# Early inputs in another order, and GpSimd beside VectorE for some of the early splits

## The chip, the cores and the metric

The kernel runs on one core of one Trainium2 chip. The metric is device time in microseconds (us); a time stated for a kernel is the median of its runs. TensorE multiplies, ScalarE and VectorE do the elementwise work, GpSimd (POOL in the profile) does very little here, and SyncE (SP) issues most of the DMA transfers.

## The reference

One decoder layer for two request groups: 256 prompt tokens and 8 sequences of 4 sample tokens, 288 tokens in all, in float32, with a model width of 4096.

```python
mod = jax.nn.silu(c) @ w_ada + b_ada
shift, scale, gate = jnp.split(mod, 3, axis=-1)
h = x * (1 + scale[:, None]) + shift[:, None]
q, k, v, z_a, u, v_b, z_b, g_a, g_b = split_cols(h @ w_in)
# A = sliding-window attention with sinks * silu(z_a)
# B = u * (masked chunk mixing of LN(v_b) + b_s) * silu(z_b)
merged = jax.nn.sigmoid(g_a) * (attn @ w_pa) + jax.nn.sigmoid(g_b) * (out_b @ w_pb)
y = merged @ w_o
x = layer_norm(ALPHA * x + gate[:, None] * y, ln_g, ln_b)
```

c has 9 rows: one for the prompt, one for each sample sequence. Part of the output are also the new key, value and v_b rows.

## The kernel before, in words

Tokens lie along the free dimension (288 columns) and the model width along the partitions, in 32 tiles of 128. The weights are streamed: a `Unit` is one DMA of up to 128 x 2048 float32 values (1 MB) on SyncE's queue into one of five `raw` buffers (L174). For the products every weight is split into a high part and a low part: for each half of a unit, ScalarE casts raw into `wH` (L182) and VectorE subtracts it from raw to get `wL` (L183), both with three buffers of 128 x 1024. The activations are split in the same way, h into `hH` (L298) and `hL` (L299). `prod` then issues three matmuls for each block of 128 x 128: wH with hH (L194), wH with hL (L195), wL with hH (L196).

The conditioning product silu(c) @ w_ada needs no split: `ada_units` multiplies the raw weights with `cT`, the transposed c, padded to 32 columns for each tile (L234). It is worked off in nine chunks of the model width, `CHUNKS` = 1, 2, 2, 2, 1, 4, 4, 8, 8 tiles. When the last conditioning unit of a chunk is done, `ada_fin` copies the result out of PSUM (`adae`, L250), transposes it on TensorE with the identity `ident` (`adaT`, L257), adds the bias `bada` (L280, L281), adds 1 to the scale (L287), modulates that chunk of x in place in the buffer `xs` (L292 for the prompt, L295 and L296 for the samples), makes hH and hL, and calls `load_x` for the next chunk of x (L270, ScalarE's queue), into the same place.

56 column tiles of w_in are worked on early ("early units", `ea` in the profile), while the conditioning still runs: as soon as a chunk of h is there, `early_units` multiplies it with the 56 column tiles and adds the PSUM result onto accumulators in SBUF (`accA`, `accB`, `xs`, `Q`). For chunk 0 the results are copied, by VectorE (L342) and ScalarE (L340) in turn; for later chunks VectorE adds (L344). PSUM holds three such results (`ps_acc`, three buffers). A unit of a chunk of n tiles holds 16 / n column tiles, so a result is complete after 3n matmuls.

The order of units is written out by `first_order`: the four conditioning units of chunk 0, two early units of chunk 0, three conditioning units of chunk 1, and so on, with two early units of the previous chunk kept for the time in which the next chunk's modulation is under way. `run` starts each unit (its DMA and its splits) two units ahead of the one whose matmuls are being issued. The framework under the kernel assigns the instructions to each engine's stream by this program order and its own estimate of when each can run, so the streams can differ from the text: matmuls of two units can stand mixed in TensorE's stream. Each engine then works its stream off in order.

After the early part come the remaining columns of w_in, attention and chunk mixing beside them, then the products with w_pa, w_pb and w_o, and the final layer normalisation, where GpSimd takes part (L869, L877).

The constants are loaded at the start on ScalarE's queue, each with its own DMA: cT, `ident`, `bada`, `lngb` (gain and bias of the last normalisation), then the first chunk of x.

Of the kernel before, what the change touches and what calls it, by code (L numbers as in the profile page):

```python
# [10 lines left out]
F32 = mybir.dt.float32  # L11
F32R = mybir.dt.float32r
AF = mybir.ActivationFunctionType
ALU = mybir.AluOpType
# [4 lines left out]
P = 128  # L19
# [91 lines left out]
def build(ctx, tc, nc, I, O):  # L111
# [17 lines left out]

    ident = const.tile([P, P], F32, name="ident")  # L130
    cT = const.tile([P, KT, 32], F32, name="cT")
    bada = const.tile([P, 96], F32, name="bada")
    lngb = const.tile([P, 2, KT], F32, name="lngb")
    gate = const.tile([P, KT, 9], F32, name="gate")
    epst = const.tile([P, 1], F32, name="epst")
    nc.scalar.dma_start(cT, I["cT"])
    nc.scalar.activation(cT, cT, AF.Silu)  # L137
    nc.scalar.dma_start(ident, I["ident"])
    nc.scalar.dma_start(bada, I["bada"])
    nc.scalar.dma_start(lngb, I["lngb"])  # L140
    nc.vector.memset(epst, EPS)

    hH = [slot(f"hH{i}", dt=F32R) for i in range(2)]
# [23 lines left out]
    class Unit:  # L167
        def __init__(self, src, body, split=True, blocks=16):
            self.src, self.body, self.split, self.blocks = src, body, split, blocks

        def start(self):
            raw = wp.tile([P, UNIT], F32, tag="raw", name="raw", bufs=RAW)
            w = self.blocks * P
            nc.sync.dma_start(raw[:, :w], self.src[:, :w])  # L174
            self.raw = raw
            self.H, self.L = [], []
            if self.split:
                for hf in range(w // 1024):
                    s = raw[:, hf * 1024:(hf + 1) * 1024]
                    h = wp.tile([P, 1024], F32R, tag="wH", name="wH", bufs=HB)  # L180
                    lo = wp.tile([P, 1024], F32R, tag="wL", name="wL", bufs=HB)
                    nc.scalar.copy(h, s)  # L182
                    nc.vector.tensor_sub(lo, s, h.bitcast(F32))  # L183
                    self.H.append(h)
                    self.L.append(lo)
# [12 lines left out]
    def run(items, ahead=2):  # L198
# [5 lines left out]
        for x in items:  # L204
            if not isinstance(x, Unit):
                x()
                continue
            while started < len(units) and started < k + 1 + ahead:
                units[started].start()
                started += 1  # L210
            x.body(x)
            k += 1
# [54 lines left out]

    def load_x(c):
        n, o = CHUNKS[c], OFFS[c]
        nc.scalar.dma_start(xs[:, 0, :n], I["xT"][:, o:o + n])  # L270

    def ada_fin(c):
        n, o = CHUNKS[c], OFFS[c]

        def modulate(blocks):
# [12 lines left out]
            for k in range(0, n, HSTEP):  # L288
                w = min(HSTEP, n - k)
                x = xs[:, 0, k:k + w]  # L290
                for i in range(w):
# [7 lines left out]
                nc.vector.tensor_sub(hL[a][:, b:b + w], x, hH[a][:, b:b + w].bitcast(F32))  # L299
            if c + 1 < len(CHUNKS):  # L300
                load_x(c + 1)
            h_done.add(c)
# [63 lines left out]
    def early_units(c):  # L366
# [17 lines left out]
        def unit(j):  # L384
            es = range(j * per, min(NE, (j + 1) * per))
            return Unit(I["we"][base + j], body_for(j, es), blocks=len(es) * n)
        return [unit(j) for j in range(count[c])]

# [501 lines left out]
    items = []  # L890
    load_x(0)

# [39 lines left out]
def layout(x_prompt, x_sample, cache_k, cache_v, c_prompt, c_sample, w_ada, b_ada, w_in, attn_sinks,  # L932
# [6 lines left out]
    c[0], c[1:9] = c_prompt[0], c_sample  # L939
    A["cT"] = f(c.reshape(32, KT, P).transpose(2, 1, 0))  # L940
    A["ident"] = np.eye(P, dtype=np.float32)
    A["bada"] = f(b_ada[0].reshape(96, P).T)
    A["gbrow"] = f(np.stack([ln_gain[0], ln_bias[0]]))
    A["lngb"] = f(np.stack([ln_gain[0], ln_bias[0]]).reshape(2, KT, P).transpose(2, 0, 1))

# [72 lines left out]
```

## Time and profile before

| | before |
|---|---|
| median of 3 runs | 3072.95 us (3072.71 to 3073.15) |
| profiled execution | 3071.9 us |
| its span | 3070.1 us |
| its mean granted TensorE clock | 0.994 |
| DMA over the span | 700.09 MB, 228 GB/s |
| VectorE busy | 1571.7 us (51%) |
| GpSimd busy | 15.4 us (1%) |

The span runs from the first to the last instruction that the profile shows. Shares are of the span. In the groups and the timeline each instruction has its engine, its line, what it writes and reads, and in brackets how long its engine stood idle before it and what ended that. A matmul counts as busy to its modelled end, so neighbours overlap: the distance of their starts is what one takes. Queue instructions (SPq, ACTq) only issue a DMA.

### The profile page before, as it was taken

The numbers are of one execution on the slowest core, as the hardware profiler recorded it, in microseconds if no ns is written. First come the engines' busy times: TensorE is split into PE (matmuls) and PEld (weight loads), VectorE is DVE, ScalarE is ACT, GpSimd is POOL, SyncE is SP. The second block draws the span as 40 slices with busy tenths as digits, with TensorE's granted clock in tenths as the row PEclk, the third lists the DMA queues.
The fourth block names the chain that finished last, engine by engine and source line by source line (L and its number), as shares of the span: only waits on it lengthen the run. The fifth ranks groups of instructions, "written<-read, shape, count | busy, mean of one in ns | idle before, by whom it ended". The sixth has DMA issues, their size and how long they took to land.

```text
span 3070.1 us, 53574 instructions
## 1 busy us (share of the span) xinstructions
PE 3030.2 (99%) x23168; PEld 2850.6 (93%) x23168; DVE 1571.7 (51%) x2262; ACT 1078.1 (35%) x1381; POOL 15.4 (1%) x14
## 2 busy tenths in 40 slices
PE   7999999999999999999999999999999999999998
PEld 6887888888999999999999999999999999999997
DVE  4777554444445545454444643444555555555555
ACT  3222223322333434343333333333444444433333
POOL 0000000000000000000000000000000000000001
PEclk9999999999999999999999999999999999999998
DMA  8888877877767565555555555666565555555552
GB/s 327 332 322 321 340 278 286 315 267 285 271 244 249 186 218 206 210 214 189 212 206 206 206 215 215 221 217 220 186 229 188 188 188 188 175 176 177 177 177 95
DMA packets 128673, 700.09 MB, mean 228 GB/s; under 512 B 14835, under 2 KB 44819, under 8 KB 49299
## 3 DMA queue, kind: packets, MB, share of 16 engines
q1 hardware_dynamic: 109584, 669.56, 60.0%
q10 hardware_dynamic: 18852, 27.10, 2.5%
q8 instruction: 182, 2.98, 0.4%
q14 instruction: 55, 0.44, 0.0%
HBM read 676.85 MB, written 19.46 MB: 227 GB/s over the span
## 4 chain that ended last, share of the span: by engine, by line
PE 95%; DVE 1%; DMA 1%; issue 0%; ACT 0%; DVEq 0%; ACTq 0%
PE in L194 13%; PE in L196 13%; PE in L195 13%; PE ea L194 8%; PE ea L195 7%; PE ea L196 7%; PE ada L234 5%; PE p L194 5%; PE y L194 5%; PE y L196 4%; PE p L196 4%; PE p L195 4%; PE y L195 4%; DVE wL L183 0%; PE pT L518 0%
## 5 line engine op out<-in xcount | busy, mean ns | idle before, releaser
L182 ACT CAST wH<-raw 128x1024 fp32r<-128x1024 f32 x848 | 884.6, 1048 | 1856.9 <-PE in L195 649.8
L183 DVE TENSOR_TENSOR wL<-raw,wH 128x1024 fp32r<-128x1024 f32 x848 | 1033.7, 1224 | 981.7 <-ACT wH L182 981.2
L194 PE MATMUL in<-hH,wH 128*128 128x288 f32 x2944 | 881.0, 299 | 0.0
L195 PE MATMUL in<-hL,wH 128*128 128x288 f32 x2944 | 869.7, 295 | 0.0
L196 PE MATMUL in<-hH,wL 128*128 128x288 f32 x2944 | 865.8, 294 | 0.0
L194 PEld LDWEIGHTS in<-hH,wH 128*128 128x128 f32 x2944 | 551.7, 187 | 23.5 <-issue 14.3
L196 PEld LDWEIGHTS in<-hH,wL 128*128 128x128 f32 x2944 | 554.4, 188 | 0.0
L195 PEld LDWEIGHTS in<-hL,wH 128*128 128x128 f32 x2944 | 552.8, 188 | 0.2
L194 PE MATMUL ea<-hH,wH 128*128 128x288 f32 x1792 | 538.8, 302 | 10.7 <-ACT hH L298 5.1
L195 PE MATMUL ea<-hL,wH 128*128 128x288 f32 x1792 | 530.2, 296 | 1.3 <-DVE hL L299 1.3
L196 PE MATMUL ea<-hH,wL 128*128 128x288 f32 x1792 | 526.0, 295 | 1.2 <-DVE wL L183 1.2
L194 PEld LDWEIGHTS ea<-hH,wH 128*128 128x128 f32 x1792 | 337.1, 188 | 53.3 <-ACT wH L182 24.4
L196 PEld LDWEIGHTS ea<-hH,wL 128*128 128x128 f32 x1792 | 338.1, 189 | 2.5 <-DVE wL L183 1.7
L195 PEld LDWEIGHTS ea<-hL,wH 128*128 128x128 f32 x1792 | 338.4, 189 | 2.1 <-DVE hL L299 1.9
L194 PE MATMUL y<-mH,wH 128*128 128x288 f32 x1024 | 303.2, 296 | 0.0
L195 PE MATMUL y<-mL,wH 128*128 128x288 f32 x1024 | 302.3, 295 | 0.0
L196 PE MATMUL y<-mH,wL 128*128 128x288 f32 x1024 | 301.1, 294 | 0.0
L234 PE MATMUL ada<-raw,cT 128*32 128x512 f32 (+2 forms) x1920 | 192.0, 516 | 11.2 <-ACT cT L137 8.3
L196 PEld LDWEIGHTS y<-mH,wL 128*128 128x128 f32 x1024 | 192.9, 188 | 0.1
L195 PEld LDWEIGHTS y<-mL,wH 128*128 128x128 f32 x1024 | 192.3, 188 | 0.1
L194 PEld LDWEIGHTS y<-mH,wH 128*128 128x128 f32 x1024 | 191.9, 187 | 0.0
L194 PE MATMUL p<-AH,wH 128*128 128x288 f32 x512 | 151.7, 296 | 0.0
(200 smaller groups left out, 2416.1 us busy)
## 6 DMA issues: line engine op xcount, KB each, us to landing
raw<-wada SPq DMA_DIRECT2D x192, 1024.0 KB, 5.2
raw<-wr SPq DMA_DIRECT2D x184, 1024.0 KB, 6.2
raw<-we SPq DMA_DIRECT2D x111, 1024.0 KB, 7.6
raw<-wo SPq DMA_DIRECT2D x64, 1024.0 KB, 4.9
raw<-wpa SPq DMA_DIRECT2D x32, 1024.0 KB, 4.9
raw<-wpb SPq DMA_DIRECT2D x32, 1024.0 KB, 4.9
gl<-gdram SPq DMA_DIRECT2D x64, 144.0 KB, 3.3
pdram<-part ACTq DMA_DIRECT2D x32, 144.0 KB, 3.9
```

The costliest lines, as they stand in the source:

```text
L182: nc.scalar.copy(h, s)
L183: nc.vector.tensor_sub(lo, s, h.bitcast(F32))
L194: mm(ps, wh, xh, start=first, stop=False)
L195: mm(ps, wh, xl, start=False, stop=False)
L196: mm(ps, wl, xh, start=False, stop=last)
L234: mm(st["ps"][32 * q:32 * q + 32, :w], cT[:, kt, :], u.raw[:, at:at + w], start=kt < 1 + paired, stop=kt >= KT - 1 - paired)
```

## The change

The conditioning vectors come as a table of 9 columns a tile (`craw`, 144 KB) in place of the padded 32 (512 KB); VectorE sets `cT` to zero, and ScalarE writes silu of the 9 columns into it. This table and x chunks 0 and 1 are issued on SyncE's queue ahead of all weight blocks. `ident`, `bada` and `lngb` come packed as one table of 288 columns (`pack`, 144 KB) on ScalarE's queue.

The x buffer is used in two halves for chunks of up to four tiles (`x_at`), so that such a chunk is loaded two chunks ahead (`next_x`), on ScalarE's queue as before. For early units (`shared=True`) the low part of the second half is made by GpSimd; that of the first half stays on VectorE. The first early unit is started only when its turn comes, after the program text of chunk 0's modulation (`before`, which calls `ensure_h(0)`).

```diff
-    ident = const.tile([P, P], F32, name="ident")
+    pack = const.tile([P, 288], F32, name="pack")
+    bada, ident = pack[:, :96], pack[:, 96:224]
+    lngb = pack[:, 224:288].rearrange("p (s k) -> p s k", s=2)
     cT = const.tile([P, KT, 32], F32, name="cT")
-    bada = const.tile([P, 96], F32, name="bada")
-    lngb = const.tile([P, 2, KT], F32, name="lngb")
...
-    nc.scalar.dma_start(cT, I["cT"])
-    nc.scalar.activation(cT, cT, AF.Silu)
-    nc.scalar.dma_start(ident, I["ident"])
-    nc.scalar.dma_start(bada, I["bada"])
-    nc.scalar.dma_start(lngb, I["lngb"])
+    craw = tmp.tile([P, KT, 9], F32, tag="t", name="craw", bufs=6)
+    nc.sync.dma_start(craw, I["cT"])
+    nc.scalar.dma_start(pack, I["pack"])
+    nc.vector.memset(cT, 0.0)
     nc.vector.memset(epst, EPS)
+    nc.scalar.activation(cT[:, :, 0:9], craw, AF.Silu)
...
                     nc.scalar.copy(h, s)
-                    nc.vector.tensor_sub(lo, s, h.bitcast(F32))
+                    eng = nc.gpsimd if self.shared and hf else nc.vector
+                    eng.tensor_tensor(lo, s, h.bitcast(F32), ALU.subtract)
...
+            if x.before:
+                x.before()
             while started < len(units) and started < k + 1 + ahead:
+                if units[started].before and started > k:
+                    break
                 units[started].start()
                 started += 1
...
-    def load_x(c):
-        n, o = CHUNKS[c], OFFS[c]
-        nc.scalar.dma_start(xs[:, 0, :n], I["xT"][:, o:o + n])
+    def x_at(c):
+        return 4 * (c % 2) if CHUNKS[c] <= 4 else 0
+
+    def load_x(c, eng=nc.scalar):
+        n, o, at = CHUNKS[c], OFFS[c], x_at(c)
+        eng.dma_start(xs[:, 0, at:at + n], I["xT"][:, o:o + n])
+
+    def next_x(c):
+
+        small = lambda k: k < len(CHUNKS) and CHUNKS[k] <= 4
+        if c + 1 < len(CHUNKS) and not small(c + 1):
+            load_x(c + 1)
+        elif small(c + 2):
+            load_x(c + 2)
...
-            if c + 1 < len(CHUNKS):
-                load_x(c + 1)
+            next_x(c)
...
-            return Unit(I["we"][base + j], body_for(j, es), blocks=len(es) * n)
-        return [unit(j) for j in range(count[c])]
+            return Unit(I["we"][base + j], body_for(j, es), blocks=len(es) * n, shared=True)
+        out = [unit(j) for j in range(count[c])]
+        if c == 0:
+            out[0].before = lambda: ensure_h(0)
+        return out
...
-    load_x(0)
+    load_x(0, nc.sync)
+    load_x(1, nc.sync)
```

The host's layout of `cT` and `pack` follows; no arithmetic moves to the host.

More of the change, by code (lines that the diff above doesn't have):

```diff
@@ L167, in build, with __init__ @@
     class Unit:
-        def __init__(self, src, body, split=True, blocks=16):
-            self.src, self.body, self.split, self.blocks = src, body, split, blocks
+        def __init__(self, src, body, split=True, blocks=16, shared=False):
+            self.src, self.body, self.split, self.blocks, self.shared = src, body, split, blocks, shared
+            self.before = None
         def start(self):
@@ L289, in modulate @@
                 w = min(HSTEP, n - k)
-                x = xs[:, 0, k:k + w]
+                x = xs[:, 0, x_at(c) + k:x_at(c) + k + w]
                 for i in range(w):
@@ L939, in layout @@
     c[0], c[1:9] = c_prompt[0], c_sample
-    A["cT"] = f(c.reshape(32, KT, P).transpose(2, 1, 0))
-    A["ident"] = np.eye(P, dtype=np.float32)
-    A["bada"] = f(b_ada[0].reshape(96, P).T)
+    A["cT"] = f(c[:9].reshape(9, KT, P).transpose(2, 1, 0))
+    lngb = np.stack([ln_gain[0], ln_bias[0]]).reshape(2, KT, P).transpose(2, 0, 1).reshape(P, 64)
+    A["pack"] = f(np.concatenate([b_ada[0].reshape(96, P).T, np.eye(P), lngb], 1))
     A["gbrow"] = f(np.stack([ln_gain[0], ln_bias[0]]))
-    A["lngb"] = f(np.stack([ln_gain[0], ln_bias[0]]).reshape(2, KT, P).transpose(2, 0, 1))
     wa = w_ada[0].reshape(KT, P, 3 * D)
```

## The prediction

> **What bounds the kernel now.** I read the page's head and the windows of the span first, to see where TensorE stops, then TensorE's waits, then the timeline of the places they name. The head gives the span and each engine's busy time; a window row gives stretch, busy time by engine, granted TensorE clock, DMA share and GB/s; a wait row gives who waited for whom, total, times and longest.
>
> ```profile
> span 3070.1 us, 53574 instructions
> PE 3030.2 (99%) x23168; PEld 2850.6 (93%) x23168; DVE 1571.7 (51%) x2262; ACT 1078.1 (35%) x1381; POOL 15.4 (1%) x14
> 0.00:25.00 25.00, 9.17 (x139) 7.06 (x139) 5.87 (x14) 6.11 (x7) 0.20 (x4) 0.89 0.95 378
> 50.00:75.00 25.00, 21.08 (x185) 17.62 (x175) 15.38 (x33) 9.05 (x14) 0.00 (x0) 0.93 0.92 358
> 75.00:100.00 25.00, 25.00 (x252) 21.79 (x251) 17.07 (x29) 4.29 (x5) 0.00 (x0) 1.00 0.72 282
> 700.00:800.00 100.00, 100.00 (x757) 88.78 (x756) 44.58 (x53) 28.32 (x27) 0.00 (x0) 1.00 0.78 282
> 800.00:3070.00 2270.00, 2258.64 (x17118) 2182.00 (x17116) 1128.28 (x1515) 848.67 (x1119) 15.21 (x10) 0.99 0.57 200
> 18.00:20.00 2.00, 0.00 (x0) 0.00 (x0) 0.51 (x2) 0.76 (x1) 0.00 (x0) 0.84 1.00 415
> 28.00:30.00 2.00, 2.00 (x11) 1.89 (x9) 0.69 (x2) 1.20 (x3) 0.00 (x0) 0.60 1.01 409
> ...
> PE ada L234 <- ACT cT L137: 8.3, 1, 8.3
> PE ea L194 <- ACT hH L298: 4.9, 1, 4.9
> ...
> PE ea L195 <- DVE hL L299: 0.9, 1, 0.9
> ...
> PE adaT L257 <- DVE adae L250: 2.9, 3, 1.6
> PE ea L194 <- DVE accB L344: 1.6, 3, 0.8
> PE ea L196 <- DVE wL L183: 1.2, 2, 0.6
> PE ea L194 <- DVE Q L344: 0.9, 2, 0.7
> ```
>
> TensorE is busy for all but 39.9 us (3070.1 - 3030.2): 15.8 before 25 us, 3.9 from 50 to 75, 11.4 after 800 (the last stage, which the change doesn't touch). That leaves 8.8 in between. So all that an early edit can win is about 28 us of idle time, plus a slow clock: 0.84 in 18 to 20 says that the half clock began near 19.36 (0.64 us of two at half rate), and 0.60 in 28 to 30 that it ended near 29.6. The first two waits are of the first 50 us; the third, for hL, of 50 to 75; the last four, together 6.6 us, of 75 to 770. Undisturbed, a product matmul takes 0.132 us (757 in the 100 us from 700).
>
> ```profile
> 2.88 0.46 ACTq L270 DMA_DIRECT2D xs<-xT  x1
> 7.15 1.06 ACT L137 ACTIVATE cT<-cT 128x1024 f32<-128x1024 f32 x1 [2.50 <-DMA cT<-cT]
> 14.93 1.08 PE L234 MATMUL ada<-raw,cT 128*32 128x128 f32 x32 [1.46 <-DMA raw<-wada]
> 17.21 0.17 DVE L287 TENSOR_SCALAR mod<-mod 128x9 f32<-128x9 f32 x1
> 19.24 1.99 ACT L182 CAST wH<-raw 128x1024 fp32r<-128x1024 f32 x2 [11.03 <-DMA raw<-we]
> 19.49 0.41 DVE L292 TENSOR_SCALAR xs<-xs,mod 128x256 f32<-128x256 f32 x1 [2.10 <-DMA xs<-xT]
> 20.32 2.36 DVE L183 TENSOR_TENSOR wL<-raw,wH 128x1024 fp32r<-128x1024 f32 x2
> 21.14 0.43 ACT L298 CAST hH<-xs 128x288 fp32r<-128x288 f32 x1
> 21.61 1.09 PE L194 MATMUL ea<-hH,wH 128*128 128x288 f32 x3 [4.86 <-ACT hH L298]
> 22.59 0.45 DVE L299 TENSOR_TENSOR hL<-xs,hH 128x288 fp32r<-128x288 f32 x1
> 23.10 0.61 PE L195 MATMUL ea<-hL,wH 128*128 128x288 f32 x1 [0.40 <-DVE hL L299]
> 23.50 0.44 PE L196 MATMUL ea<-hH,wL 128*128 128x288 f32 x1
> 23.74 0.44 PE L195 MATMUL ea<-hL,wH 128*128 128x288 f32 x1
> ```
>
> In the timeline (start, duration, engine, line; in brackets the idle time before, and its end) the last conditioning unit is multiplied by 16.01 and the modulation vector stands at 17.38, but x arrives at 19.49. The first weight block of the early products lands just before (19.24), so its two casts stand ahead of hH on ScalarE, and two low parts ahead of hL on VectorE. The product stream flows from 23.10 on, one matmul in 0.24 us (23.50 to 23.74) at the half clock.
>
> **The change part by part: the start.** cT of 512 KB, three tables (144 KB by their shapes) and x of 144 KB shared ScalarE's queue: 800 KB. Now c of 144 KB, x chunk 0 of 144 and chunk 1 of 288 lead SyncE's queue and the pack of 144 KB is ScalarE's: 720 KB. At 415 GB/s (18 to 20) the 80 KB saved are 0.2 us, so the weight blocks land about when they did; the three transfers ahead delay SyncE's first weight issue by some 1.4 us (0.46 each, as the x issue took on ScalarE), during which 576 KB move (1.4 us at that rate): nothing lost.
>
> Silu shrinks from 1024 to 288 columns and starts when 144 KB have landed, not 512, with four DMA issues fewer before the table load on ScalarE; the added memset of cT stands on an idle VectorE. The 8.3 us wait for cT falls, but then the first weight block is late, and TensorE still ends the conditioning when the fourth block has landed (14.93), some 0.3 us sooner at most, and what comes next hides that. The vectors are ready near 17.1, and x is there: the three x operations took 0.74 us (19.49 to 20.23), hH 0.43, hL 0.45, so both parts of h stand near 18.8.
>
> Next late is the first weight block. It came 4.3 us after the fourth conditioning block (19.24 - 14.93), though 1 MB at 415 GB/s takes 2.5. Bounds: 17.2 by the rate, 19.2 as seen; I take 18.9, near the row. Its first cast (1.0) ends at 19.9, TensorE starts at 20.0 instead of 21.61, and its low part (half of 2.36) is there near 21.2. Six products that need no low part (two in each of three PSUM tiles) fill that time at 0.24 each; before, three were done when the stream flowed from 23.10. Gain 23.10 - 21.2 = 1.9, plus 3 x 0.24 = 0.7: 2.6. The clock came back 6.5 us after the stream began to flow; if that moves along, the gain is whole, if it stays at 29.6, half of it (1.3). From this I take off 0.2 for VectorE held up in the first group (below): **-2.4, bounds -0.4 to -4.1**.
>
> Chunk 1's x, and from then on a load two chunks ahead, removes no wait: x chunk 0 is the one x load that any engine waited for (2.10). Holding the first early unit back until its turn defers casts that waited 11.03 us for its data anyway; SyncE's order of blocks stays.
>
> **GpSimd's low parts.** 111 early units have a second half (issues of 1 MB below), so 111 low parts of 1.22 us leave VectorE: 135 us. GpSimd has no such operation of this size; the nearest are those of the last stage, 576 wide.
>
> ```profile
> raw<-we SPq DMA_DIRECT2D x111, 1024.0 KB, 7.6
> L183 DVE TENSOR_TENSOR wL<-raw,wH 128x1024 fp32r<-128x1024 f32 x185 | 224.3, 1222 | 109.6 <-ACT wH L182 109.5
> 3047.56 5.48 POOL L869 TENSOR_TENSOR d<-d,fin 128x576 f32<-128x576 f32 x4 [3047.12 <-ACT fin L850]
> 3056.24 6.52 POOL L877 TENSOR_TENSOR d<-d,us 128x576 f32<-128x576 f32 x4
> 3057.55 1.40 DVE L869 TENSOR_TENSOR d<-d,rp 128x576 f32<-128x576 f32 x2
> 3059.61 1.90 DVE L877 TENSOR_TENSOR d<-d,us 128x576 f32<-128x576 f32 x1
> 3063.48 0.75 DVE L877 TENSOR_TENSOR d<-d,us 128x576 f32<-128x576 f32 x1
> ```
>
> 5.48 / 4 = 1.37 for 576, by width 2.4 us for 1024 (2.9 by the second row). A half block feeds TensorE for 24 matmuls, 3.2 us at 0.132; with three buffers a low part has two such halves, 6.4 us, less the cast's 1.05: hidden, also the later return of the raw buffer by about 1.2 us, as DMA is at 0.72 in 75 to 100. Without that cover it would cost 1.2 us a unit.
>
> The trace shows a price: VectorE's d<-d,us, both inputs in SBUF, takes 0.75 with GpSimd quiet and 1.90 beside it, while d<-d,rp, one input in PSUM, keeps 0.70 beside the same GpSimd work. So a VectorE operation on two SBUF inputs (wL, hL) waits out GpSimd's; the adds from PSUM don't, unless queued behind one. [...]
>
> ```profile
> 61.33 2.35 DVE L183 TENSOR_TENSOR wL<-raw,wH 128x1024 fp32r<-128x1024 f32 x2
> 63.60 0.82 DVE L299 TENSOR_TENSOR hL<-xs,hH 128x288 fp32r<-128x288 f32 x2
> 252.87 6.56 DVE L344 TENSOR_TENSOR accA<-accA,ea 128x288 f32<-128x288 f32 x16
> 259.35 2.35 DVE L183 TENSOR_TENSOR wL<-raw,wH 128x1024 fp32r<-128x1024 f32 x2
> ```
>
> At chunk 1, hL stands behind two low parts and TensorE waits 0.9 for it. With the second on GpSimd (62.5 to 64.9) hL, whose turn comes at 62.5, is held to 64.9, 1.3 later than 63.60. Bounds: 1.1 gained if hL gets in first, 1.8 lost at GpSimd's 2.9; I take **+1.3**, since a GpSimd operation already in line, like VectorE's above, goes next. Later boundaries have two early units kept to cover them. In the one-block chunk near 250, 16 adds (6.56, 0.41 each) plus two low parts (2.4) exceed the 6.3 of its 48 matmuls: VectorE is the limit, and 1.2 a unit leaves it. Of the 6.6 us of waits for VectorE after 75 I take **-2.0** (bounds 0 and -6.6), and for holds elsewhere **+0.5** (0 to the slow rival's).
>
> Sum: -2.4 + 1.3 - 2.0 + 0.5 = -2.6. The profiled execution took 3071.9 (span 3070.1), which gives 3069.3; it lies 1.05 below the median of 3072.95, so the median becomes **3070.4**.
>
> **The rivals.** *Hidden anyway:* if the scheduler still puts both casts ahead of hH and the block lands at 19.2, hH stays near 21.1 and only hL comes sooner, 22.1 for 23.0: 0.9, of which a clock that returns where it did leaves 0.4. With +1.3 at chunk 1 and as much relief, the time is 3072.5. For it: x and the block arrived within 0.3 us of each other; against it: hL's place behind two low parts goes.
>
> *Faster:* all of the relief (-6.6), hL first (-1.1) and the block by the rate (-4.1) would be -11.8; the last, with 70% of the relief (-4.6) and chunk 1 neutral, is -8.7: 3064.3. Against: several bounds must hold. A clock that never falls would save another 3.2 (half of the 6.5 us): TensorE's pause shrinks from 4.9 to some 3.4 us, but the clock fell 2.6 us into it (16.76 to 19.36), so I give it 5 in 100. [...]
>
> *Slower:* the shared port decides. Chunks 0 to 4 hold 28 units (4 + 7 + 7 + 7 + 4, less one half), where a PSUM tile is full every 0.4 or 0.8 us (3 or 6 matmuls) and three tiles cover 1.2 to 2.4. A held low part keeps VectorE from its adds for up to 2.4 + 1.2 = 3.6 us: 1.2 to 2.4 of stall. If half of the units meet it at 1.2, that is +16.8; with the gains (-4.4), +12.4: 3085.4. It decides from 0.38 us a unit on ((6.1 + 4.4) / 28, where the time is 0.2% up). Against: casts in steady state come 3.2 us apart, longer than GpSimd's 2.4, so most low parts don't meet.
>
> **How the numbers follow.** 0.2% is 6.1 us, about what a measurement of this kernel can tell from no change. Forecast 0.47 (own range 3067.5 to 3072.5), hidden anyway 0.20, faster 0.20, slower 0.13. Faster by 0.2% (under 3066.8): 0.20; slower (over 3079.1): 0.11; the rest, 0.69, within. The range 3064.0 to 3076.0 leaves out about half of the faster rival and most of the slower.
>
> **What would show it.** Right: the wait for hH in the first 25 us under 3.5 us, first product near 20.0, the half clock over by 27, x never waited for, GpSimd low parts near 2.4 us, VectorE wL rows of over 1.22 beside them, hL of chunk 1 late. Wrong: TensorE waits for accA, accB or Q growing by several us between 60 and 300 (slower); a first block landing near 17.2 or no half clock (faster); or an instruction order on ScalarE with both casts still ahead of hH.

## The result and the profile after

The changed kernel takes 3088.98 us (median of 6 runs, 3087.83 to 3091.37) against 3072.83 for the kernel before (6 runs, 3071.20 to 3075.66): 1.0056 times as long, 95% interval 1.0045 to 1.0067. It is slower by 16 us; 3070.4 was forecast. The profiled execution took 3091.06 us, with a span of 3089.2.

The head of the page after:

```profile
span 3089.2 us, 53711 instructions
PE 3039.1 (98%) x23168; PEld 2855.0 (92%) x23168; DVE 1458.4 (47%) x2152; ACT 1077.6 (35%) x1381; POOL 284.8 (9%) x125
```

The span grew by 19.1 us (3089.2 - 3070.1). TensorE's idle time grew by 10.2 of it (50.1 against 39.9), but its busy time grew too, by 8.9 (3039.1 - 3030.2), with the same 23168 matmuls. So a list of waits can explain only half of the loss. Two things lengthen the busy time: another order of TensorE's instructions, 4.1 us (below), and a lower granted clock, 0.9925 on the mean for 0.9940 before, which by an estimate is 4.8 us of work at the full clock (0.0075 x 3089.2 less 0.0060 x 3070.1). VectorE was relieved by 113 us (1571.7 - 1458.4), as intended, and nothing of it shows in the time.

The windows after (stretch, busy time by engine, granted clock, DMA share, GB/s), with the stretches that the prediction showed and two later ones:

```profile
0.00:25.00 25.00, 10.31 (x141) 8.13 (x141) 4.86 (x13) 5.49 (x7) 2.70 (x5) 0.87 0.93 367
24.00:26.00 2.00, 2.00 (x12) 1.82 (x10) 0.64 (x3) 0.94 (x3) 0.96 (x1) 0.66 1.06 442
28.00:30.00 2.00, 2.00 (x14) 1.63 (x13) 0.85 (x2) 1.29 (x4) 1.47 (x1) 1.00 1.01 417
50.00:75.00 25.00, 18.90 (x121) 16.64 (x114) 14.14 (x29) 8.14 (x12) 4.77 (x2) 0.80 0.79 298
200.00:340.00 140.00, 137.26 (x956) 106.97 (x955) 76.95 (x162) 33.06 (x36) 37.35 (x15) 1.00 0.79 311
880.00:1012.00 132.00, 127.78 (x950) 121.22 (x949) 41.46 (x60) 38.10 (x37) 43.62 (x19) 0.99 0.72 247
```

The first 25 us got better, 50 to 75 got worse (18.90 busy for 21.08, clock 0.80 for 0.93). The stage from 880 to 1012, where the last of the nine chunks is worked on, has 4.2 us of idle time that the prediction didn't look for. TensorE's waits after, from the stretches 0 to 50, 50 to 75, 75 to 300, 300 to 500 and 830 on (line waiting, what it waited for, total, times, longest):

```profile
PE ea L196 <- ACT hH L315: 3.4, 1, 3.4
...
PE ea L196 <- ACT wH L183: 3.0, 1, 3.0
PE ea L197 <- DVE hL L316: 1.7, 1, 1.7
...
PE ea L196 <- DVE accB L360: 3.7, 6, 1.4
PE ea L196 <- DVE Q L360: 2.7, 4, 1.1
...
PE ea L196 <- DVE accB L360: 2.2, 1, 2.2
...
PE ea L196 <- ACT wH L183: 2.8, 2, 2.4
PE ea L198 <- DVE wL L185: 1.5, 2, 0.7
```

Against before, TensorE's waits for accB and Q between 75 and 300 grew from 2.5 to 6.4 us in all, and there are two new places: one wait of 2.2 for accB, at 361, and those for wH and wL after 830, where before there were none in the early products.

The timeline after, at the places that decide (start, duration, engine, line; in brackets the idle time before and its end; dots stand for rows left out):

```profile
17.74 0.33 PE L263 MATMUL adaT<-pack,adae 128*128 128x128 f32 x1 [0.41 <-DVE adae L256]
20.06 1.04 ACT L183 CAST wH<-raw 128x1024 fp32r<-128x1024 f32 x1 [14.67 <-DMA raw<-we]
21.01 0.43 ACT L315 CAST hH<-xs 128x288 fp32r<-128x288 f32 x1
21.49 1.09 PE L196 MATMUL ea<-hH,wH 128*128 128x288 f32 x3 [3.42 <-ACT hH L315]
...
61.18 2.37 POOL L185 TENSOR_TENSOR wL<-raw,wH 128x1024 fp32r<-128x1024 f32 x1 [19.02 <-ACT wH L183]
61.49 3.15 DVE L185 TENSOR_TENSOR wL<-raw,wH 128x1024 fp32r<-128x1024 f32 x1
64.56 0.81 DVE L316 TENSOR_TENSOR hL<-xs,hH 128x288 fp32r<-128x288 f32 x2
65.06 0.40 PE L197 MATMUL ea<-hL,wH 128*128 128x288 f32 x1 [1.67 <-DVE hL L316]
...
254.85 1.05 PE L240 MATMUL ada<-raw,cT 128*32 128x512 f32 x2
255.83 0.40 PE L196 MATMUL ea<-hH,wH 128*128 128x288 f32 x1
...
357.82 0.18 DVE L313 TENSOR_TENSOR xs<-xs,mod 128x32 f32<-128x32 f32 x1
357.90 2.37 POOL L185 TENSOR_TENSOR wL<-raw,wH 128x1024 fp32r<-128x1024 f32 x1 [5.42 <-ACT wH L183]
357.93 2.39 DVE L312 TENSOR_TENSOR xs<-xs,mod 128x32 f32<-128x32 f32 x1
361.57 0.40 PE L196 MATMUL ea<-hH,wH 128*128 128x288 f32 x1 [2.17 <-DVE accB L360]
...
996.18 2.47 POOL L185 TENSOR_TENSOR wL<-raw,wH 128x1024 fp32r<-128x1024 f32 x1 [8.34 <-ACT wH L183]
998.67 12.28 SPq L175 DMA_DIRECT2D raw<-we  x6
1006.06 1.99 ACT L183 CAST wH<-raw 128x1024 fp32r<-128x1024 f32 x2 [9.96 <-DMA raw<-we]
```

Five things are to be read here. **Start:** the weight block lands at 20.06, later than before (19.24), and its cast still stands ahead of hH. **Hold, chunk 1:** a low part on VectorE that starts 0.31 us after GpSimd's takes 3.15 us, where the mean of all 737 is 1.23, hL follows it, TensorE waits 1.67. **Order:** a group of only two conditioning matmuls between products takes 0.98 us (254.85 to 255.83). **Hold, 357.93:** an addition of 128 x 32 takes 2.39 us where the one before it took 0.18; it ends as GpSimd's operation does (360.32 and 360.27), and the adds into accB stand behind it. **Late return:** GpSimd's low part ends at 998.65, SyncE issues the next weight block into the freed buffer at 998.67, and the cast that needs a block starts after 9.96 us of idle ScalarE. The shared port of the recorded texts is the author's name for the cause of such holds; the runs show the holds, and no port.

The DMA traffic from 975 to 1012 after, in 40 slices of 0.92 us:

```profile
GB/s 0 151 242 452 369 349 50 0 159 239 417 406 71 0 35 106 239 416 295 312 225 19 0 0 16 214 266 365 352 363 337 337 416 416 407 425 425 425 434 416
```

In the 22nd to 25th slice (994.4 to 998.1) hardly anything moves, just before that issue. The transfers weren't slow; they were waiting for a buffer.

### The profile page after: what moved, and what is told of

The parts are those of the page before. It is cut to its first block, busy times and chain, and to the rows that moved or that the text cites. A ratio compares the mean times of both kernels' runs of the same rounds, so it can differ in the third digit from the quotient of the medians.

```text
span 3089.2 us, 53711 instructions
## 1 busy us (share of the span) xinstructions
PE 3039.1 (98%) x23168; PEld 2855.0 (92%) x23168; DVE 1458.4 (47%) x2152; ACT 1077.6 (35%) x1381; POOL 284.8 (9%) x125
## 4 chain that ended last, share of the span: by engine, by line
PE 94%; DMA 2%; DVE 2%; ACT 1%; issue 0%; SPq 0%; POOL 0%; ACTq 0%; DVEq 0%
PE in L196 13%; PE in L198 12%; PE in L197 12%; PE ea L196 8%; PE ea L198 7%; PE ea L197 7%; PE ada L240 5%; PE p L196 4%; PE y L196 4%; PE y L198 4%; PE p L198 4%; PE p L197 4%; PE y L197 4%; DMA raw<-we 1%; DVE wL L185 1%; ACT wH L183 1%
## 5 line engine op out<-in xcount | busy, mean ns | idle before, releaser
L185 DVE TENSOR_TENSOR wL<-raw,wH 128x1024 fp32r<-128x1024 f32 x737 | 905.0, 1231 | 971.4 <-ACT wH L183 970.9
L196 PE MATMUL ea<-hH,wH 128*128 128x288 f32 x1792 | 540.9, 303 | 18.5 <-DVE accB L360 5.9
L185 POOL TENSOR_TENSOR wL<-raw,wH 128x1024 fp32r<-128x1024 f32 x111 | 269.4, 2427 | 778.8 <-ACT wH L183 705.7
L888 POOL TENSOR_TENSOR d<-d,fin 128x576 f32<-128x576 f32 x5 | 6.9, 1400 | 2018.0 <-ACT fin L869 2018.0
```

The costliest lines, as they stand in the source:

```text
L185: eng.tensor_tensor(lo, s, h.bitcast(F32), ALU.subtract)
L196: mm(ps, wh, xh, start=first, stop=False)
L888: eng.tensor_tensor(z, z, bc(rp if eng is nc.vector else rstd, 1, (P, 2, T)), ALU.mult)
```

## The experiments

For each kernel the trace gives the start of every early product (5376 in each). The table is worked out from these: how many us a product starts later than the product at the same place in the start-only kernel of the first experiment, for the products that this one starts at the time (us) in the head; "end" compares the last instruction. With the same code, differences of up to 2.4 us at a single place were seen (column 22, e10 and e13). The last column is the median less that of the kernel before in the same comparison. Each row is one execution: those of e8 and e14 (3076.88 and 3076.78 us) are some 4 us below their medians, that of the changed kernel is 2 us above.

| kernel | 22 | 62 | 68 | 202 | 250 | 311 | 376 | 904 | 1011 | end | median above before |
|---|---|---|---|---|---|---|---|---|---|---|---|
| before | 0.5 | 1.2 | 1.1 | 1.5 | 1.4 | 0.5 | 0.6 | 0.6 | 0.5 | -0.2 | 0 |
| changed | 0.4 | 1.5 | 3.2 | 5.1 | 3.1 | 9.9 | 11.4 | 11.4 | 18.2 | 19.0 | 16.2 |
| e1 start only | 0 | 0 | 0 | 0 | 0 | 0 | 0 | 0 | 0 | 0 | -0.6 |
| e3 changed, GpSimd without raw | 0.0 | 1.5 | 3.2 | 3.1 | 0.8 | 7.6 | 8.6 | 8.7 | 8.7 | 8.5 | 7.2 |
| e8 GpSimd in last chunk only | 0.0 | 0.2 | 0.2 | 0.5 | 0.5 | -1.0 | -1.1 | -1.1 | 5.1 | 4.8 | 8.7 |
| e9 start only, changed order | 0.0 | 1.4 | 1.1 | -0.4 | -1.4 | 6.4 | 6.1 | 6.1 | 6.1 | 6.2 | 7.7 |
| e10 changed, first order | 1.2 | 1.5 | 3.3 | 4.3 | 2.8 | 1.3 | 7.5 | 7.5 | 16.0 | 16.4 | 14.8 |
| e11 as e10, without raw | 0.1 | 0.8 | 0.5 | 0.2 | -1.2 | -2.8 | 1.8 | 1.8 | 1.8 | 2.2 | 2.9 |
| e13 as e10, one unit back | -1.2 | -1.5 | 0.5 | 1.9 | 0.5 | -1.1 | 2.4 | 2.4 | 8.3 | 8.4 | 10.1 |
| e14 as e10, eight units back | -0.4 | -0.3 | -0.7 | -1.2 | -2.7 | -4.2 | -2.2 | -2.2 | 5.0 | 4.7 | 8.6 |
| e15 as e14, last chunk back | -0.1 | -0.2 | 0.0 | -0.4 | -1.9 | -3.4 | 0.1 | 0.1 | 0.1 | 0.2 | 0.7 |

"First order" is the order of TensorE's instructions in the start-only kernel, "changed order" that in the changed kernel.

**Halving the change (e1, e2).** e1 takes the changed kernel with all low parts on VectorE; e2 takes the kernel before with only the GpSimd low parts.

```diff
 # e1
-            return Unit(..., blocks=len(es) * n, shared=True)
+            return Unit(..., blocks=len(es) * n, shared=False)
 # e2 (against before)
-                    nc.vector.tensor_sub(lo, s, h.bitcast(F32))
+                    eng = nc.gpsimd if self.shared and hf else nc.vector
+                    eng.tensor_tensor(lo, s, h.bitcast(F32), ALU.subtract)
```

> The changed kernel with every low part on VectorE again; the early inputs, the packed constants, the x halves and the held first unit stay. Theory A (all of the loss is GpSimd's; the start is worth the 2.2 to 2.5 us by which the changed kernel led until 51 us): 3070.5, that is 2 to 3 us below before, and the 19.1 us by which the profiled executions differ gone. Rival B (the early inputs or the held first unit cost later what they gain at first): 3075 or more. Rival C (GpSimd and the start each carry a part): 3078 to 3082.

> The kernel before with the second low part of each early unit on GpSimd and nothing else. Theory A: before plus 18 to 21 us, 3091 to 3094, as the start's gain is missing. Rival B: within 3 us of before. Rival C: before plus 5 to 10.

e1: 3071.96 us, ratio 1.0001 (0.9992 to 1.0011). e2: 3090.61, ratio 1.0061 (1.0046 to 1.0076). The start is worth nothing in the end, and GpSimd's low parts, with all that they bring about, are the whole loss.

**What GpSimd reads, and where (e3, e4).** In e3 GpSimd subtracts wH from itself, so its half of the low parts is zero, and the raw buffer is free after the cast; its operation then takes 1.92 us instead of 2.43. In e4 GpSimd serves chunks 0 and 1 alone.

```diff
 # e3
-                    eng.tensor_tensor(lo, s, h.bitcast(F32), ALU.subtract)
+                    eng.tensor_tensor(lo, h.bitcast(F32) if eng is nc.gpsimd else s, h.bitcast(F32), ALU.subtract)
 # e4
-            return Unit(..., shared=True)
+            return Unit(..., shared=c <= 1)
```

> The changed kernel, but GpSimd subtracts wH from itself (same size, two inputs in SBUF, same engine, the low part comes out as zero), so that the raw buffer is free when ScalarE's second cast is done and not when GpSimd is. Theory of the late release (a raw buffer comes back 1.2 us or more later, and where blocks are fetched one behind another the next one is late): the steps between 340 and 375, near 911 and from 985 to 1011 us go, 5 to 9 us: 3080 to 3084. Rival, the shared port: these steps stay, since the port is as busy: 3088 to 3090. Neither touches the steps at 51 to 77 and 222 to 311 us by more than 2 us.

> The changed kernel with GpSimd's low parts in chunks 0 and 1 alone. By the shared port (VectorE's low part of chunk 1 took 3.15 us behind GpSimd's, hL came later): the step of 4.6 us at 51 to 77 us stays and all others go: start only plus 3 to 5 us, near 3075. Rival, that the step at 77 is a late block (the wait for a cast grew from 1.6 to 3.0 us) that comes from the changed start: it is in the start-only kernel too, and this one equals it within 1.5 us.

e3: 3079.79, ratio 1.0024 (1.0014 to 1.0033), more than half of the loss gone. The table says where: nothing after 904 is left, and most of what came before is. The edit also shortens GpSimd's operation, and the two effects are not separated. e4: 3074.92, ratio 1.0008 (0.9999 to 1.0018): 2.4 us by medians, hardly told from nothing. Here hL itself met GpSimd, as forecast for chunk 1 (2.62 us instead of 0.45), and in the profiled execution (the fastest of ten, 3071.76) the delay was given back by 311: it lags behind e1 by 1.8 us at 202 and by 0.2 at 311.

**Is it TensorE's order? A control that failed (e5, e6, e7).** TensorE's instructions stand in another order in the changed kernel's trace than in e1's, though their program text is the same: the framework's scheduler orders them anew once low parts are on GpSimd. e5 (start only), e6 (changed) and e7 (as e3) keep each conditioning matmul and the first product of each early unit in the order of the program text.

```diff
-                        mm(st["ps"][32 * q:32 * q + 32, :w], cT[:, kt, :], u.raw[:, at:at + w], ...)
+                        tc.keep_in_program_order(
+                            mm(st["ps"][32 * q:32 * q + 32, :w], cT[:, kt, :], u.raw[:, at:at + w], ...))
...
-        mm(ps, wh, xh, start=first, stop=False)
+        i = mm(ps, wh, xh, start=first, stop=False)
+        if unit.shared_kind and m == 0:
+            tc.keep_in_program_order(i)
```

> The start-only kernel (no low part on GpSimd), with TensorE's stream held to the program order of the units: no conditioning matmul is moved into an early unit any more. A group of conditioning matmuls of eight or fewer cost about 1.0 us whether it held two or eight, so whole units should save up to 4 us; what is lost is work that filled a wait. Expected 3067 to 3073; if filling waits was worth more than whole groups, 3075 or more. It is the control for the next one.

> The changed kernel (GpSimd's low parts in all chunks), TensorE's stream held to the same order of units as in the control. Theory of the order (the step of 5.8 us at 222 to 311 us is conditioning matmuls that stand in pairs between products because the assigned order changed with the engine of the low part): that step shrinks to under 2 us, and the distance to the control is 10 to 13 us, not the 17 to 18 between the changed and the start-only kernel. Rival, the shared port (VectorE held up in the short groups): the step of 4 to 6 us stays at that place, and the distance stays at 16 to 19.

> As the one before, but GpSimd subtracts wH from itself (its low parts come out as zero), so that the raw buffer is free at the cast. Order and late release are both gone; what is left against the control is the shared port and GpSimd's own 2.4 us: 1 to 4 us by the account so far. If it is 8 or more, neither order nor release was the larger part.

e5: 3078.94, ratio 1.0024 (1.0015 to 1.0033); e6: 3083.34, 1.0038 (1.0023 to 1.0053); e7: 3073.71, 1.0007 (0.9998 to 1.0017). The control alone loses 7 us: conditioning matmuls that the scheduler moves into waits are worth more than unbroken groups (from 100 to 311 us TensorE stands idle for 13.3 us in e5, for 5.5 in e1). So the pair says little on the order. It does say that GpSimd costs 4.4 us on top when both follow this rule, and that without raw this is gone.

**The last chunk alone (e8).** `shared=c == 8` in place of `shared=True`.

> The changed kernel with GpSimd's low parts in the last chunk alone (28 units). TensorE's order equals that of the start-only kernel. By the late release: steps of 1 to 2 us near 911 and of 4 to 6 us from 985 to 1011, nothing before 850: start only plus 5 to 8, near 3078. By the rival, that the last steps follow from something earlier: start only plus under 2.

3080.75, ratio 1.0031 (1.0019 to 1.0042): 8.7 us with 28 low parts of 111. The windows from 880 to 1012 of six kernels (e1, e3, e8, e9, e14, e15 in this order; second number TensorE's busy time, POOL's is the last before the clock) show what goes with it:

```profile
880.00:1012.00 132.00, 132.00 (x1001) 126.38 (x1001) 66.20 (x99) 40.49 (x39) 0.00 (x0) 1.00 0.73 260
```
```profile
880.00:1012.00 132.00, 132.00 (x1000) 126.31 (x1000) 43.36 (x78) 40.64 (x39) 37.19 (x20) 1.00 0.73 262
```
```profile
880.00:1012.00 132.00, 128.43 (x955) 121.87 (x955) 43.23 (x76) 38.40 (x37) 43.93 (x19) 0.99 0.72 252
```
```profile
880.00:1012.00 132.00, 132.00 (x1001) 126.38 (x1000) 66.31 (x98) 40.55 (x39) 0.00 (x0) 1.00 0.73 263
```
```profile
880.00:1012.00 132.00, 128.56 (x948) 122.00 (x947) 42.73 (x75) 37.34 (x36) 43.49 (x18) 0.97 0.73 253
```
```profile
880.00:1012.00 132.00, 132.00 (x1001) 126.38 (x1000) 66.18 (x98) 40.51 (x39) 0.00 (x0) 1.00 0.72 259
```

TensorE is busy throughout wherever GpSimd is quiet here (e1, e9, e15), and also where GpSimd works but does not hold raw (e3). Where GpSimd reads raw (e8, e14, and the changed kernel with 127.78) it stands idle for 3.4 to 4.2 us. The table's step after 904 is larger, 6.2 to 7.2 in these three, because the clock falls behind the pause: from 985 to 1015 it is 1.00 in e1, 0.94 in e8 and in the changed kernel, 0.89 in e14. By an estimate (the share lost of these 30 us) that is 1.8 us more, 3.3 in e14. So it isn't GpSimd's work as such that costs here, it is the buffer that it holds (but for the 0.5 us by which e3's operation is shorter).

**The order by itself (e9 to e11).** e9 gives the start-only kernel the changed kernel's order of TensorE's instructions, e10 the changed kernel the start-only one's; e11 is e10 with e3's edit. The order is set by chaining the matmuls (`REC` lists them as they are written) of the eight stretches that differ, without a semaphore. The other engines nearly keep their order: going by the names of what they write and read, 37 of VectorE's first 917 instructions and 4 of ScalarE's first 341 differ between e9 and e1.

```diff
+    for block in PE_ORDER:
+        at = [i for a, n in block for i in range(a, a + n)]
+        for i, j in zip(at, at[1:]):
+            tc.add_manual_dep(REC[j], REC[i].name, mybir.DependencyInfo(
+                mybir.DependencyClass.NoSync, mybir.DependencyReason.DATA), reason="order")
```

> The start-only kernel (every low part on VectorE), with TensorE's stream forced into the order that the changed kernel has; that order differs from its own in 780 of 21859 places, in eight stretches, all before 400 us. Theory of the order: it alone carries most of the loss before 900 us, 6 to 11 us against start only, 4 to 6 of them at 222 to 311 us, and nothing from 904 to 1011: 3078 to 3083. Rival (GpSimd's duration and the shared port): within 2 us of start only, 3070 to 3074.

> The changed kernel, GpSimd's low parts in all chunks, with TensorE's stream forced into the order of the start-only kernel. Theory of the order: the loss before 900 us falls from 11 to under 4 us against start only, the late release from 904 to 1011 stays at 6 to 7: 3077 to 3082. Rival: no better than the changed kernel by more than 3 us, 3086 to 3089.

> As the one before, but GpSimd subtracts wH from itself (its low parts come out as zero), which frees the raw buffer at the cast. What is left against start only is the shared port and GpSimd's 2.4 us, less what VectorE is relieved of: -3 to +2 us, 3068 to 3074. Should it be 5 or more above, the port is a third cause of size.

e9: 3079.25, ratio 1.0025 (1.0015 to 1.0034). e10: 3086.40, 1.0045 (1.0029 to 1.0062). e11: 3074.51, 1.0009 (1.0000 to 1.0019). The order alone, with no instruction on GpSimd, costs 7 us, and the step from 250 to 311 (7.8 us in e9, 6.8 in the changed kernel) belongs to it, since e10 doesn't have it. In e1's timeline some conditioning matmuls of that stretch stand in long groups:

```profile
247.66 1.92 PE L240 MATMUL ada<-raw,cT 128*32 128x512 f32 x14
249.51 0.40 PE L196 MATMUL ea<-hH,wH 128*128 128x288 f32 x1
```

Fourteen take 1.85 us (247.66 to 249.51), two took 0.98 in the changed kernel. Counted over the same 523 products, from about 215 to 310 us, e1's 160 conditioning matmuls stand in 13 groups and take 22.9 us to the next product, the changed order's 160 stand in 18 groups and take 27.0, in the changed kernel as in e9. That is 4.1 of the step, and it is busy time (a group costs some 0.86 us for each eight matmuls begun, as the last section shows, and the changed order begins 28 eights where e1 begins 23); from 200 to 340 e9 also has 1.7 us more idle time than e1 (135.46 us busy in 140 against 137.18), and from 202 to 311 its products take 1.7 us longer in all, for a reason that wasn't looked for.

But e10 isn't 7 us faster than the changed kernel, it is 1.4 (14.8 for 16.2 above before): a step of 6.2 us appears between 311 and 376. The expectation of e3 put a step at this place on raw; yet e11, which frees raw, has most of it (4.6). The timelines of e10 and then e11 show why:

```profile
349.17 2.39 POOL L206 TENSOR_TENSOR wL<-raw,wH 128x1024 fp32r<-128x1024 f32 x1 [5.51 <-ACT wH L204]
349.26 2.35 DVE L334 TENSOR_TENSOR xs<-xs,mod 128x32 f32<-128x32 f32 x1
352.98 0.61 PE L134 MATMUL ea<-hH,wH 128*128 128x288 f32 x1 [3.30 <-DVE accB L381]
```
```profile
345.12 1.94 POOL L206 TENSOR_TENSOR wL<-wH 128x1024 fp32r<-128x1024 f32 x1 [6.12 <-ACT wH L204]
345.21 1.90 DVE L334 TENSOR_TENSOR xs<-xs,mod 128x32 f32<-128x32 f32 x1
```

The same small addition as in the changed kernel at 357.93, held by the low part of the same unit. TensorE waits 3.30 in e10 and its clock falls: the first product after it takes 0.61 us instead of 0.40. The windows from 340 to 380 (clock third from the end), e10 and then the changed kernel:

```profile
340.00:380.00 40.00, 36.15 (x246) 30.34 (x248) 20.31 (x43) 11.38 (x15) 11.83 (x5) 0.91 0.71 268
```
```profile
340.00:380.00 40.00, 37.29 (x279) 32.41 (x278) 21.85 (x47) 11.75 (x14) 12.41 (x5) 1.00 0.87 340
```

By an estimate the clock costs e10 3.6 us here (0.09 of 40), as much as the wait itself. The changed kernel waits 2.17 us at this place, keeps the full clock and loses 1.5. In e11 (wait 2.8, clock 0.96) and in e13 below (1.8 and 0.96) wait and clock add up to the step in the same way: 4.4 for 4.6 and 3.4 for 3.5.

**Exchange of halves (e12).** As e10, with the first half's low part on GpSimd and the second on VectorE (`self.shared and not hf`), so that VectorE would return the buffer.

> The changed kernel in the start-only kernel's order of TensorE's stream, with GpSimd making the low part of each unit's first half and VectorE that of the second, so that VectorE gives the raw buffer free. Theory of the late release: the steps from 904 to 1011 us are under 2 us, as VectorE's low part ends 1.2 us or more sooner than GpSimd's would: 3071 to 3076. Rival, the shared port: VectorE's second low part, ready 1.05 us after GpSimd has begun, stands behind it each time, ends no sooner than GpSimd's would have, and the steps stay at 5 or more: 3077 or more.

3082.25, ratio 1.0034 (1.0021 to 1.0047), above the 3071 to 3076 that the late return had promised. The timeline shows that the edit didn't do what it was for:

```profile
898.92 1.99 ACT L204 CAST wH<-raw 128x1024 fp32r<-128x1024 f32 x2 [7.83 <-DMA gdram<-xs]
900.05 2.38 POOL L206 TENSOR_TENSOR wL<-raw,wH 128x1024 fp32r<-128x1024 f32 x1 [9.68 <-ACT wH L204]
900.95 2.56 DVE L206 TENSOR_TENSOR wL<-raw,wH 128x1024 fp32r<-128x1024 f32 x1 [3.97 <-ACT wH L204]
```

The casts end at 900.91; VectorE's low part would follow in 1.22 us, but it stands behind GpSimd's and ends at 903.51, 2.60 after the cast, as late as GpSimd's own would be (2.47). The run separates nothing: held like this, VectorE gives the buffer back as late as GpSimd would. The loss fell after 904 here too (-0.7 to 9.0 us).

**One unit, eight units, the last chunk (e13 to e15).** All three are e10 with units given back to VectorE: the one that met the addition at 349; this and the seven others that met VectorE on its way to h at a chunk boundary; these and the whole last chunk.

```diff
-            return Unit(..., shared=True)
+            return Unit(..., shared=(c, j) != (5, 9))                 # e13
+            return Unit(..., shared=(c, j) not in HELD)               # e14
+            return Unit(..., shared=c < 8 and (c, j) not in HELD)     # e15
+HELD = {(1, 0), (1, 6), (2, 0), (2, 4), (2, 5), (3, 0), (3, 1), (5, 9)}
```

> As the run with GpSimd's low parts in the first order (3086.4 us, span 3086.7), except that one unit, the tenth of the sixth chunk, has both its low parts made by VectorE: 110 low parts on GpSimd instead of 111. That unit's GpSimd operation (349.17 to 351.56 us) stands beside a 128x32 add of x on VectorE that took 2.35 us instead of 0.18, and TensorE then waited 3.30 us for an add into accB. Shared port: that add takes 0.18 again, the wait of 3.30 us goes, the lag behind the start-only kernel no longer grows by 6.3 us between 345 and 360, and the time is about 3080 (3079 to 3082). Late return of the raw buffer as the cause of that stretch: one unit's buffer comes back 1.2 us sooner, so at most 1.2 us are won: 3085 to 3086. No change at all (3086.4): the stretch has a third cause.

> As the one before, and seven more units are given back to VectorE whose low part on GpSimd met an operation on the way to h or a first low part at a chunk boundary (the first and last of the second chunk, three of the third, two of the fourth): 103 low parts on GpSimd. Port: the steps of the lag at 61 (about 2 us) and between 110 and 200 us (about 1) go too, and VectorE's relief is left alone until 900 us: 2 to 3 us ahead of the start-only kernel at 376 us. The late return in the last chunk stays (8.9 us): 3076 to 3079. If VectorE's relief was never there, the lag at 376 us is 0 or above, and the time 3079 to 3082. If these units meet others instead (every low part of VectorE that falls beside GpSimd's waits), 3082 or more.

> As the one before, and in the last of the nine chunks VectorE makes all low parts: GpSimd has 75 of them, none after some 815 us. If what was left is the late return of the raw buffer in the last chunk, the 8.9 us after 900 us go, and the relief of 2 to 3 us stays: 3068 to 3071, ahead of both kernels. If the relief was never there: 3071 to 3074, as the start-only kernel (3072.0). If the loss after 900 us comes from something that does not hang on the last chunk's low parts: 3076 or more.

e13: 3082.23, ratio 1.0039 (1.0025 to 1.0053). By medians this one unit of 111 is worth 4.7 us (10.1 above before for 14.8), but the intervals of the two overlap, so the step in the table is the firmer measure: between 311 and 376 it shrinks from 6.2 to 3.5. That is more than the 1.2 of the buffer would explain, and less than the 6.3 that was expected of the hold. The timeline shows what is left of the place:

```profile
348.39 0.18 DVE L334 TENSOR_TENSOR xs<-xs,mod 128x32 f32<-128x32 f32 x1
349.10 0.40 PE L134 MATMUL ea<-hH,wH 128*128 128x288 f32 x1 [1.78 <-DVE accB L381]
```

The addition takes 0.18 again and the wait falls from 3.30 to 1.78, not to nothing: VectorE now makes that low part itself, and the adds into accB queue behind it.

e14: 3080.73, ratio 1.0029 (1.0018 to 1.0041), where 3076 to 3079 was expected. The steps from 62 to 202 are gone (to the hold or to the buffers of these units: e11, which frees raw and leaves GpSimd's operations in place, lacks most of them too, 0.2 at 202 for 4.3 in e10) and the kernel runs 4.2 us ahead at 311, of which 2.0 go at the wait near 346 and 7.2 in the last chunk. e15: 3072.86, ratio 1.0002 (0.9993 to 1.0010): the last chunk's 7.9 us are gone, as the late return says, but the 3.4 us of lead at 311 are spent at 376, where 3068 to 3071 hung on their lasting. So no version is faster than the kernel before by more than a measurement can tell.

## Why the prediction was wrong

**What the 16 us are.** By medians above before: e15 stands at 0.7, the last chunk adds 7.9 (e14), the eight boundary units add 6.2 (e10), the order adds 1.4 (changed kernel; the intervals of 1.0029 to 1.0062 and 1.0045 to 1.0067 overlap, so this last step isn't told from nothing). Taken in the other way, the order alone is 7.7 (e9) and GpSimd on top 8.5. The two ways differ mostly at the boundary near 350: 1.5 us are lost there in the changed kernel, 6.2 in e10, where TensorE waits longer and the clock falls behind the wait. Both ways have the same three causes, and the sum held none of them at its size. Part of each comes as a slower clock after the pause and not as idle time.

**The step that failed first** is the term set to nothing: "hidden, also the later return of the raw buffer by about 1.2 us, as DMA is at 0.72 in 75 to 100". It named 1.2 us a unit as the price without cover; the last chunk loses some 8 us over 28 units, so the cover fails at a few of them. The reading was wrong twice: the place was not the one where the loss fell, and a DMA share below 1 was taken for slack. In the last chunk the share is about 0.73 in every kernel above, with or without loss, and what is missing to 1 is not free time: the queue is waiting for a buffer. The DMA queue's own waits from 850 to 1020, after and then in e1:

```profile
SPq L175 <- POOL wL L185: 89.8, 23, 4.9
SPq L175 <- DVE wL L185: 53.9, 23, 8.2
```
```profile
SPq L175 <- DVE wL L185: 116.2, 22, 6.0
```

In 144 of 170 us after, and in 116 in e1, the next transfer waits until a low part gives a buffer back; after, it is GpSimd's in 90 of them. So these waits tell whose release the transfers hang on, but not the price, since e1 waits nearly as long and loses nothing. The price stands in TensorE's waits for wH and wL after 830 (2.8 and 1.5 us, before none) and in the clock behind them (1.8 us by the estimate above): 6.1 of the 6.8 us after 904 in the table. That a buffer's return goes round the loop of issue, landing and cast more than once, and so adds up to a wait of 2.4 us at one place, would fit but wasn't measured by itself.

**The step that was missing:** every term took TensorE's order as given and only asked what would be late. The prediction looked for the scheduler in one place, hH behind the casts. An operation that changes engine changes the order that the scheduler works out for the others; this order alone, without any work on GpSimd, costs 7 us (e9).

**Chunk 1, +1.3:** right in place and kind, and too small. The changed kernel loses 2.1 us there against e9, which has the same order and no GpSimd operation (3.2 - 1.1 at 68). It was the low part on VectorE that was held (3.15), and hL behind it. TensorE waits 1.7 us for hL where e9 waits 0.8, and from 62 to 75 its clock is 0.83 for 0.96 (1.7 us by an estimate, 0.13 of 13).

**"Later boundaries have two early units kept to cover them", +0.5:** this failed. In the changed kernel five VectorE operations on the way to h, or in front of it, are held by 1.8 us or more, and at 357.93 even an addition of 0.18 us carries the adds into accB with it, past the cover. The eight such units of the first order cost 6.2 us in medians there (intervals of 1.0029 to 1.0062 and 1.0018 to 1.0041, which overlap) and 9.7 at 376 in the profiles; before 311 this is not separated from the sooner return of their buffers, near 350 e11 shows the hold without it (the addition held for 1.90 us, TensorE waiting 2.8). The prediction had read the hold from two rows before (1.90 us beside GpSimd, 0.75 without), and it is there after: 0.18 becomes 2.39, until GpSimd's instruction is over. The port that *slower* names as its cause is shown by no run; what they showed in its place is VectorE operations held beside GpSimd's low part: 3.15 us at 61.49, 2.39 at 357.93, 2.35 in e10, and in e11 1.90. The error was to apply the hold to the operations that were already late, and not to the small ones that others queue behind.

**Relief, -2.0:** it was there, and larger: 3.4 us of lead in e15 and 4.2 in e14 at 311, gathered from 202 on where VectorE was said to be the limit. But it doesn't reach the end. At the next boundary, near 346, TensorE comes sooner to the same place and waits 1.8 for accB, and the lead shrinks to 2.2 (e14, clock 1.00 from 340 to 380) or to nothing (e15, clock 0.96, 1.6 us by the same estimate). Why VectorE isn't ahead there too is open.

**Start, -2.4:** the wait for hH fell from 4.9 to 3.4 and the half clock (0.50 granted from 20 to 24 us, before from 20 to 28) ended near 25.4 instead of 29.6 (0.66 from 24 to 26, then 1.00), as listed for the case that it is right; x was never waited for. But the wait is shorter for another reason than the one given: TensorE transposes at 17.74 instead of 16.43, as the conditioning blocks land later and not 0.3 sooner (the fourth is multiplied from 16.24, before from 14.93), and hH is done only 0.1 us sooner. That this shorter pause meets the listed sign is luck. The first product came at 21.49, not at 20.0: the first weight block landed 0.8 us later than before instead of 0.3 sooner, and a cast still stood before hH, as *hidden anyway* had it. What was gained was gained by the clock: e1 leads the kernel before by 2.1 us at 30 and 2.9 at 38, by 1.1 to 1.5 from 50 to 250, by 0.6 or less from 311 on, and at the end not at all. Where it goes wasn't tried.

**The rivals.** *Slower* was nearest in time (3085.4) and named one of the three causes. Its sum was not the right one: it charged adds in 14 of 28 units of the first chunks with 1.2 us each (there are 27 with a second half, as two units are half ones, which makes it 16.2 and not 16.8), and the hold costs a few places on the way to h instead, while most of the loss came from the last chunk and the order. *Hidden anyway* describes the start alone.

## What to carry to other kernels

When an operation moves to a slower engine, list everything that it holds until it ends, an input buffer above all, and price it by giving it back sooner in an experiment: here neither the DMA share nor the queue's waits told a stage with a loss from one without. Where an operation of one engine is held beside another engine's, look for the smallest operations that much queues behind: here the addition of 0.18 us took 2.21 more beside GpSimd's low part, and a low part of 1.22 took 1.93 more. Where TensorE pauses for 2 to 3 us, look at the clock behind the pause as well: in some of these executions it cost as much again (in e10 3.6 us by an estimate, for a wait of 3.30). And compare the instruction order of the engines that you did not touch before you trust a sum of waits: if a scheduler orders them, it has answered the change too.

## What the runs showed of the hardware

Groups of conditioning matmuls (32 columns wide, 512 moving elements) between products cost, from the start of the group to the next product and without idle time: two, four or six 0.98 to 0.99 us, eight 1.00, 14 or 16 1.85, 22 or 24 2.71, 32 3.57 (e1 and the changed kernel, 215 to 310 us). So the cost goes in steps of some 0.86 us for each eight begun, and a group of two costs as much as one of eight.

In the clock record the granted share falls to 0.50 in two stretches of the kernel before ahead of the last stage, of 10.24 us (from 19.4) and 3.41 (from 56.9), and in four of the changed kernel, of 6.83 (from 18.5), 6.83 (from 56.1), 3.41 (from 66.3) and 3.41 (from 1008.4). Whether one follows a pause is not settled by its length: waits of 1.8 us were followed by a clock of 1.00 in e14 and of 0.96 in e15, one of 2.17 in the changed kernel by 1.00 and one of 2.8 in e11 by 0.96 (340 to 380 us).

GpSimd's subtraction of 128 x 1024 with two inputs took 2.427 us on the mean of 111, as was worked out by width from the last stage's rows, and 1.923 when both inputs were the same buffer:

```profile
L185 POOL TENSOR_TENSOR wL<-raw,wH 128x1024 fp32r<-128x1024 f32 x111 | 269.4, 2427 | 778.8 <-ACT wH L183 705.7 <-DMA pdram<-part 61.0 <-PE ada L240 9.8
```
```profile
L185 POOL TENSOR_TENSOR wL<-wH 128x1024 fp32r<-128x1024 f32 x111 | 213.4, 1923 | 824.7 <-ACT wH L183 804.5 <-PE ada L240 10.8 <-PE ea L197 6.6
```

The first is the changed kernel's group, the second e3's.
